# The attention part of w_out as pairs of 64-row products into two banks, both added by VectorE

## The chip, the cores and the metric

The kernel runs on one core of one Trainium2 chip. The metric is the device time of one execution in microseconds. Engines are named as in the profile: PE (TensorE), PEld (its weight loads), DVE (VectorE), ACT (ScalarE), POOL (GpSimd) and SP (SyncE, which issues nearly all the DMAs here; SPq is its queue).

## The reference

One transformer block on 1024 tokens of width 1024: a modulated norm, a projection, dilated attention beside a gated delta rule, `w_out`, and a gated FFN.

```python
def reference(x, c, w_ada, b_ada, norm_attn_g, w_in, rel_bias, conv_w, ..., w_out, norm_ffn_g, w_gate, w_up, w_down, final_norm_g):
    ...
    y_attn = _dilated_attention(...)     # 1024 x 512
    y_delta = _gated_deltanet(...)       # 1024 x 512
    y = jnp.concatenate([y_attn, y_delta], axis=-1) @ w_out[l]
    x = x + g1 * y
    h = _rmsnorm(x, norm_ffn_g[l]) * (1.0 + sc2) + sh2
    y = (jax.nn.silu(h @ w_gate[l]) * (h @ w_up[l])) @ w_down[l]
    x = x + g2 * y
    return _rmsnorm(x, final_norm_g)
```

The change touches only the rows of `w_out` that meet `y_attn`: a product of 512 inputs, 1024 outputs and 1024 tokens.

## The kernel before, in words

Everything is held transposed: features on the 128 partitions, tokens along the free axis, in two halves of 512 tokens (`hf`). A float32 product is made of three products of split operands (high part by high, high by low, low by high), so one result of 128 features by 512 tokens over 512 inputs takes 4 blocks of 128 rows times 3, that is 12 products, added up in one PSUM bank.

While the last attention heads are still at work, `out_delta` multiplies the delta half of `w_out`, adds the residual `x`, and writes the partial results to the DRAM buffer `xp`. Then comes the stage that is changed: for each half `hf` and each feature block `d` of 0 to 7 it loads the weight slab with `wsplit` (a DMA into `wr`, its high part by ACT into `wh`, its low part by POOL into `wl`), loads `xp` into the tile `x2[d, hf]`, runs the 12 products with `gemm` (line 589) and adds the result times the gate into `x2` on DVE (line 1560). The banks come in turn from the tags `g` and `s`, two of each. ACT squares `x2` (lines 1568, 1571), and POOL, or for the last two DVE, adds the squares up in `acc` (line 1572).

Two results behind, `x2_turn` (line 1483) turns `x2` back with four 128x128 transposes on PE into a bank of tag `t`; ACT copies it to `xt` (line 1485), and SP stores it (line 1486). After the eighth result of a half, `norm2` sums `acc` over the partitions (`ssq`, line 1521), takes root and reciprocal (`r`), and spreads them with a product of ones (`rsb`, line 1528, from `dg`, line 1524). For half 0 `normed2` (line 1534 on DVE, 1537 on ACT) and `h2_split` (line 1503 on ACT, 1504 on DVE) then make the operands H11 and H21 of the FFN, while PE is at half 1. Two weight slabs of the FFN's first product are loaded early into `er` (line 1543), in the buffers of `wr`.

The order on each engine is made ahead of the run by a list scheduler from priorities and dependencies; `urgent()` raises a priority, and `issue_after` sets one instruction behind another. Each engine then runs its list strictly in order and waits on semaphores.

Of the kernel before, what the change touches and what calls it, by code (L numbers as in the profile page):

```python
# [13 lines left out]
ALU = mybir.AluOpType  # L14
# [4 lines left out]
P = 128  # L19
# [63 lines left out]
def build(tc, I, out):  # L83
    nc = tc.nc
# [17 lines left out]
    def const(shape, name, dt=F32):  # L102
        return cp.tile(shape, dt, name=name, tag=name)

    def urgent():
        return tc.high_priority(offset=6000)
# [10 lines left out]
        out=tri, in_=tri, pattern=[[1, P]], compare_op=ALU.is_ge, fill=0.0,  # L117
# [28 lines left out]
    def gbank(name):  # L146
        return psb(name, "g", 2)
# [4 lines left out]
    def tbank(name):  # L152
        return psb(name, "t", 2)

    def abank(name):
        return psb(name, "a", 1)

    def ybank(name):
        return psb(name, "y", 1)
# [24 lines left out]
    mod = const([P, 48], "mod")  # L184
# [5 lines left out]
    for j in range(3):  # L190
        n = min(HALF, 1152 - HALF * j)
        ps = tbank(f"ps_R{j}")
# [30 lines left out]
    def wsplit(src, n, name, eng=None, hurry=True):  # L223
        raw = wp.tile([P, slot], F32, name=f"wr_{name}", tag="wr", bufs=3)
        hi = wp.tile([P, slot], F32R, name=f"wh_{name}", tag="wh", bufs=5)
        lo = wp.tile([P, slot], F32R, name=f"wl_{name}", tag="wl", bufs=5)
        with urgent() if hurry else ExitStack():
            nc.sync.dma_start(raw[:, :n], src)
            nc.scalar.copy(hi[:, :n], raw[:, :n])  # L229
            (eng or nc.gpsimd).tensor_tensor(  # L230
                out=lo[:, :n], in0=raw[:, :n], in1=hi[:, :n].bitcast(F32), op=ALU.subtract
            )
        return hi, lo
# [110 lines left out]
    for k in range(KT):  # L344
# [6 lines left out]
        if k == 0:  # L351
            for i in range(KT):
# [4 lines left out]
                out=G1[:, 0:1], in0=mod[:, 8:9], scalar=1.0, in1=ga[:, 0:1], op0=ALU.add, op1=ALU.mult  # L357
            )
            scaled(0, 1)
        for hf in range(2):  # L360
            cs = slice(hf * HALF, (hf + 1) * HALF)
            nc.scalar.mul(hh[k][:, cs], xts[k][:, cs], G1[:, k : k + 1])
            nc.vector.scalar_tensor_tensor(
                out=hl[k][:, cs], in0=xts[k][:, cs], scalar=G1[:, k : k + 1], in1=hh[k][:, cs].bitcast(F32),
                op0=ALU.mult, op1=ALU.subtract,
# [69 lines left out]
    for i in range(2):  # L435
        ps = aux[:, P * i : P * i + P]
# [47 lines left out]
    for hf in range(2):  # L484
        cs = slice(hf * HALF, (hf + 1) * HALF)
# [19 lines left out]
        if hf == 0:  # L505
            nc.vector.memset(pmod[3][:, 0:64], 0.0)
            for j in range(2):
                for k in range(KT):
                    w0 = slice((k % 4) * P, (k % 4 + 1) * P)
# [5 lines left out]
    for j in range(4):  # L515
        cs = slice(0, T if j < 2 else HALF)
# [42 lines left out]
    last, taken = [None], [None]  # L559
# [21 lines left out]
    def gemm(ps, slabs, mh, ml, cs):  # L581

        n = len(slabs) * 4 * 3
        i = 0
        for (wh, wl), k0 in slabs:
            for k4 in range(4):
                w0 = slice(k4 * P, (k4 + 1) * P)
                for a, b in ((wh, mh), (wh, ml), (wl, mh)):
                    last[0] = nc.tensor.matmul(ps, a[:, w0], b[k0 + k4][:, cs], start=(i == 0), stop=(i == n - 1))  # L589
                    i += 1  # L590
                yield 0.64
# [28 lines left out]
    def run(gen):  # L620
        for _w in gen:
            pass


    for q in range(2):
        ps = gbank(f"g_qd{q}")
        cs = slice(HALF, T)
# [26 lines left out]
    def v4(t):  # L654
        return t.rearrange("p (g n h) -> p g n h", g=2, n=8)
# [5 lines left out]
    for g in range(2):  # L661
        nc.vector.tensor_tensor(
            out=v4(t1)[:, g], in0=ba[:, 1, g], in1=dtb[:, 4 * g : 4 * g + 4].unsqueeze(1).to_broadcast([P, 8, 4]), op=ALU.add
# [602 lines left out]
    yh, yl = {}, {}  # L1266
# [198 lines left out]
    ps = abank("g2t")  # L1465
# [13 lines left out]
    def x2_turn(d, hf, t, bank=None):  # L1479

        ps = (bank or (abank if (hf, d % 3) == (1, 0) else tbank))(f"x2t{d}_{hf}")
        for b in range(4):
            nc.tensor.transpose(ps[:, b * P : (b + 1) * P], t[:, b * P : (b + 1) * P], ident)
        xt = px.tile([P, 4, P], F32, name=f"xt2_{d}_{hf}", tag="m", bufs=5)
        nc.scalar.copy(xt.rearrange("p b d -> p (b d)"), ps)
        nc.sync.dma_start(
            _.x2[hf][:, :, d * P : (d + 1) * P].rearrange("b p d -> p b d"), xt
        )
# [12 lines left out]
    def h2_split(name, k, src, lo_eng, copy=None):  # L1501
        hi, lo = HB[name][k]
        (copy or nc.scalar.copy)(hi, src)
        lo_eng.tensor_tensor(out=lo, in0=src, in1=hi.bitcast(F32), op=ALU.subtract)
# [27 lines left out]
    def normed2(d, hf):  # L1532
        t = x2[d, hf]
        nc.vector.scalar_tensor_tensor(
            out=t, in0=t, scalar=G2[:, d : d + 1], in1=rs, op0=ALU.mult, op1=ALU.mult
        )
        nc.scalar.activation(t, t, AF.Identity, bias=mod[:, 24 + d : 25 + d])

    def slab_early(s):
        raw = wp.tile([P, slot], F32, name=f"er{s}", tag="wr", bufs=3)  # L1540
        hi = pe.tile([P, HALF], F32R, name=f"eh{s}", tag="eh", bufs=2)
        lo = pe.tile([P, HALF], F32R, name=f"el{s}", tag="el", bufs=2)
        nc.sync.dma_start(raw, I["wg"][0, s])
        nc.scalar.copy(hi, raw)
        nc.gpsimd.tensor_tensor(out=lo, in0=raw, in1=hi.bitcast(F32), op=ALU.subtract)
        return hi, lo

    for hf in range(2):
        cs = slice(hf * HALF, (hf + 1) * HALF)
        if hf == 1:  # L1550
            acc = px.tile([P, HALF], F32, name="acc2_1", tag="m", bufs=5)
            slabs0 = [slab_early(s) for s in range(2)]
        for d in range(KT):
            slabs = [(wsplit(I["wo"][d, 0], 512, f"wo{d}_0_{hf}"), 0)]
            t = x2[d, hf]
            nc.sync.dma_start(t, _.xp[2 * d + hf])
            ps = (gbank, sbank)[d % 2](f"wo{d}_0_{hf}")
            run(gemm(ps, slabs, yh, yl, cs))
            with urgent():
                nc.vector.scalar_tensor_tensor(  # L1560
                    out=t, in0=ps, scalar=mod[:, 16 + d : 17 + d], in1=t, op0=ALU.mult, op1=ALU.add,
                )
            behind.append((d, hf, t))
            if len(behind) > 2:
                with tc.issue_after(last[0].ins):
                    x2_turn(*behind.pop(0))
            if d == 0:
                nc.scalar.activation(acc, t, AF.Square)
            else:
                sq = px.tile([P, HALF], F32, name=f"sq2_{hf}_{d}", tag="m", bufs=5)  # L1570
                nc.scalar.activation(sq, t, AF.Square)
                (nc.vector if d > 5 else nc.gpsimd).tensor_tensor(out=acc, in0=acc, in1=sq, op=ALU.add)
        if hf == 1:
            break
        while behind:
            x2_turn(*behind.pop(0))
        rs = norm2(hf, acc, ybank(f"ssq2_{hf}"), abank(f"rsb2_{hf}"))
        for d in range(KT):
            normed2(d, hf)
            h2_split(("H11", "H21")[d // 4], d % 4, x2[d, 0], nc.vector)  # L1580
# [181 lines left out]
    for k in range(4):  # L1762
# [3 lines left out]
        t = px.tile([P, HALF], F32, name=f"t2_{k}", tag="m", bufs=5)  # L1766
# [260 lines left out]
```

## Time and profile before

| | us |
|---|---|
| median of 3 runs (lowest to highest) | 1386.41 (1386.33 to 1388.37) |
| the profiled execution | 1385.31 |
| its span, first to last instruction | 1383.3 |
| granted TensorE clock, mean | 0.995 |
| DMA, share of 16 engines | 54.7% |
| changed stage, half 0: first product to the last one of `d` 7 | about 684 to 709 |
| changed stage, half 1: last product of the additions | about 739 |

A row of the timeline gives start, duration, engine, line, operation, output<-inputs, shape (rows*columns of the array, then partitions x elements), how many in a row were merged, and in brackets how long the engine was idle before and what ended the wait. Records of PE overlap: a product's duration holds its way through the array, and the distance between two starts is what one costs. A group's row gives count, busy time and mean, then idle time ahead and its releasers. Rows of stretches give the busy time and count of each engine, the granted clock, and the DMAs' share.

### The profile page before, as it was taken

How to read it: one execution, taken by the hardware profiler on the slowest of the kernel's cores; microseconds unless marked ns; L12 is line 12 of the kernel's file. 1: busy time of each engine (PE TensorE's matmuls, PEld its weight loads, DVE VectorE, ACT ScalarE, POOL GpSimd, SP SyncE). 2: the span in 40 equal slices, each digit the busy share in tenths (PEclk: the TensorE clock that was granted, in tenths of full speed). 3: DMA queues.
4: the chain of work that ended last, by engine and by line, in shares of the span. 5: the costliest groups of instructions: out<-in, count | busy, mean ns of one | idle time of the engine just before them, and what ended most of it. 6: DMA issues, size and time to landing. Idle time of an engine off the chain costs nothing.

```text
span 1383.3 us, 24383 instructions
## 1 busy us (share of the span) xinstructions
PE 1336.5 (97%) x8984; PEld 1105.9 (80%) x8984; DVE 875.4 (63%) x1678; ACT 659.7 (48%) x1285; POOL 268.4 (19%) x250
## 2 busy tenths in 40 slices
PE   8998999999999999999999999999999999999998
PEld 5777887888889877687877788888888888888876
DVE  3688583657847242766248978666675776474497
ACT  4497514347233454775168633333333333454455
POOL 2345303324213434542261000000000000000000
PEclk9999899999999999999999999999999999999999
DMA  8665574475362546531675346445453665765585
GB/s 313 228 191 171 163 212 159 138 221 164 120 175 82 170 139 178 150 100 66 211 242 168 113 154 209 142 160 175 151 177 123 218 215 183 251 226 193 191 272 192
DMA packets 169871, 245.64 MB, mean 178 GB/s; under 512 B 32566, under 2 KB 73831, under 8 KB 169752
## 3 DMA queue, kind: packets, MB, share of 16 engines
q1 hardware_dynamic: 169752, 244.08, 54.7%
q8 instruction: 71, 1.16, 0.3%
q14 instruction: 48, 0.39, 0.1%
HBM read 181.27 MB, written 67.48 MB: 180 GB/s over the span
## 4 chain that ended last, share of the span: by engine, by line
PE 71%; DVE 14%; DMA 5%; ACT 4%; issue 3%; POOL 2%; SPq 0%; POOLq 0%; DVEq 0%; ACTq 0%
PE wua L1621 9%; PE wga L1621 8%; PE X L1821 6%; PE wgc L1621 4%; PE wuc L1621 4%; PE g_a L589 4%; PE wo L589 3%; PE Z L1821 3%; PE Y L1821 2%; PE wub L1621 2%; PE wgb L1621 2%; PE y L1372 2%; PE g_va L615 2%; DVE tm L898 2%; PE f L250 2%
## 5 line engine op out<-in xcount | busy, mean ns | idle before, releaser
L1611 DVE TENSOR_TENSOR wl_db<-wr_db,wh_db 128x512 fp32r<-128x512 f32 x77 | 53.0, 691 | 67.2 <-ACT wh_db L1610 67.0
L1610 ACT CAST wh_db<-wr_db 128x512 fp32r<-128x512 f32 x77 | 47.4, 620 | 86.3 <-PE X L1821 37.8
L1331 DVE CUSTOM_DVE_ANT_0 X<-S,ng 128x512 f32<-128x512 f32 (+3 forms) x64 | 36.6, 587 | 60.9 <-PE S L1328 53.7
L1338 POOL TENSOR_SCALAR X<-X,sc 128x128 f32<-128x128 f32 (+7 forms) x64 | 48.6, 762 | 90.5 <-DVE sc L1337 77.5
L1821 PE MATMUL X<-wl_db,wh_da 128*128 128x512 f32 x160 | 62.4, 390 | 0.3 <-DVE wl_db L1611 0.3
L1821 PE MATMUL X<-wh_db,wl_da 128*128 128x512 f32 x160 | 62.3, 389 | 0.0
L1821 PE MATMUL X<-wh_db,wh_da 128*128 128x512 f32 x160 | 62.2, 389 | 0.0
L1336 ACT ACTIVATE X<-X,sc 128x128 f32<-128x128 f32 (+7 forms) x64 | 49.4, 773 | 26.7 <-DVE sc L1331 25.1
L1611 DVE TENSOR_TENSOR wl_da<-wr_da,wh_da 128x512 fp32r<-128x512 f32 x77 | 52.9, 687 | 3.5 <-ACT wh_da L1610 3.5
L1610 ACT CAST wh_da<-wr_da 128x512 fp32r<-128x512 f32 x77 | 47.4, 616 | 14.0 <-DMA wr_da<-ao_d 7.1
L589 PE MATMUL wo<-yh,wh_wo 128*128 128x512 f32 x128 | 52.0, 406 | 0.0
L589 PE MATMUL g_a<-hh,wh_a 128*128 128x512 f32 x128 | 51.4, 402 | 0.0
L589 PE MATMUL wo<-yh,wl_wo 128*128 128x512 f32 x128 | 51.1, 399 | 0.0
L589 PE MATMUL wo<-yl,wh_wo 128*128 128x512 f32 x128 | 50.6, 395 | 0.5 <-DVE yl L1439 0.5
L589 PE MATMUL g_a<-hl,wh_a 128*128 128x512 f32 x128 | 50.6, 396 | 0.0
L589 PE MATMUL g_a<-hh,wl_a 128*128 128x512 f32 x128 | 50.4, 394 | 0.0
L1351 PE MATMUL tr<-ident,X 128*128 128x128 f32 x288 | 44.1, 277 | 4.3 <-ACT et L1356 1.6
L1610 ACT CAST wh_wg_s<-wg_s 128x512 fp32r<-128x512 f32 x33 | 20.6, 623 | 56.1 <-PE wuc L1621 23.8
L1351 PEld LDWEIGHTS tr<-ident,X 128*128 128x128 f32 x288 | 32.6, 140 | 15.3 <-POOL X L1338 6.8
L1610 ACT CAST wh_wg<-wr_wg 128x512 fp32r<-128x512 f32 x31 | 19.3, 621 | 46.2 <-PE wua L1621 18.9
L1610 ACT CAST wh_wu_s<-wu_s 128x512 fp32r<-128x512 f32 x33 | 20.4, 621 | 43.6 <-PE wga L1621 17.2
L230 POOL TENSOR_TENSOR wl_wo<-wr_wo,wh_wo 128x512 fp32r<-128x512 f32 x24 | 31.8, 1326 | 48.5 <-ACT wh_wo L229 44.3
(554 smaller groups left out, 4341.9 us busy)
## 6 DMA issues: line engine op xcount, KB each, us to landing
wm<-in_wada SPq DMA_DIRECT2D x44, 512.0 KB, 6.4
wr_da<-ao_d SPq DMA_DIRECT2D x77, 256.0 KB, 2.9
wr_wu<-in_wu SPq DMA_DIRECT2D x50, 256.0 KB, 2.8
wr_wg<-in_wg SPq DMA_DIRECT2D x48, 256.0 KB, 2.9
ao_d<-a SPq DMA_DIRECT2D x44, 256.0 KB, 2.5
wr_wd<-in_wdn SPq DMA_DIRECT2D x44, 256.0 KB, 3.0
wr_db<-wt_d SPq DMA_DIRECT2D x44, 256.0 KB, 2.7
ao_d<-as SPq DMA_DIRECT2D x33, 256.0 KB, 2.0
```

The source lines that it names most:

```text
L230: (eng or nc.gpsimd).tensor_tensor(out=lo[:, :n], in0=raw[:, :n], in1=hi[:, :n].bitcast(F32), op=ALU.subtract)
L250: nc.tensor.matmul(first[bank], a[:, w0], b[k][:, cs], start=(k == 0 and n_ == 0), stop=(k == KT - 1 and n_ == 2))
L589: last[0] = nc.tensor.matmul(ps, a[:, w0], b[k0 + k4][:, cs], start=(i == 0), stop=(i == n - 1))
L615: last[0] = nc.tensor.matmul(ps[:, :n], a[k][:, ts_], b[:, w0], start=(i == 0), stop=(i == 23))
L1331: nc.vector.tensor_tensor_reduce(out=X[:, c0:c1], in0=ps[:, 0 : c1 - c0], in1=ng[:, u + c0 : u + c1], scale=1.0, scalar=(3e38 if m is None ...
L1336: nc.scalar.activation(X[:, 0:nk], X[:, 0:nk], AF.Exp, scale=-1.0, bias=m, accum_out=sc[:, 2:3])
L1338: nc.gpsimd.tensor_scalar(out=X[:, 0:nk], in0=X[:, 0:nk], scalar1=sc[:, 3:4], scalar2=0.0, op0=ALU.mult, op1=ALU.add)
L1351: nc.tensor.transpose(ps[:, (kb - c0) * P : (kb - c0 + 1) * P], X[:, kb * P : kb * P + P], ident)
L1610: nc.scalar.copy(hi, src)
L1611: (eng or nc.vector).tensor_tensor(out=lo, in0=src, in1=hi.bitcast(F32), op=ALU.subtract)
L1621: nc.tensor.matmul(ps, a[:, w0], b, start=(first and k == 0 and n_ == 0), stop=(k == 3 and n_ == 2), skip_group_check=True,)
L1821: nc.tensor.matmul(bank[b], a[:, ts_], w, start=(first and n_ == 0), stop=(last and n_ == 2), skip_group_check=True,)
```

## The change

Each 128-row product becomes two of 64 rows: rows 0 to 63 of weight and operand into a bank of tag `g`, rows 64 to 127 into a bank of tag `s`, in turn. Each bank ends with the sum over half of the inputs, and DVE adds both to `x2`, one after the other. Count by count: 192 products become 384, 16 additions on DVE become 32, and each result holds two of the four banks, not one.

```diff
+    def gemm_rows(two, slab, mh, ml, cs):
+
+        wh, wl = slab
+        i = 0
+        for k in range(4):
+            w0 = slice(k * P, (k + 1) * P)
+            for a, b in ((wh, mh), (wh, ml), (wl, mh)):
+                for e in range(2):
+                    rows = slice(64 * e, 64 * e + 64)
+                    last[0] = nc.tensor.matmul(
+                        two[e], a[rows, w0], b[k][rows, cs], start=(i == 0), stop=(i == 11)
+                    )
+                i += 1
...
             t = x2[d, hf]
             nc.sync.dma_start(t, _.xp[2 * d + hf])
-            ps = (gbank, sbank)[d % 2](f"wo{d}_0_{hf}")
-            run(gemm(ps, slabs, yh, yl, cs))
-            with urgent():
-                nc.vector.scalar_tensor_tensor(
-                    out=t, in0=ps, scalar=mod[:, 16 + d : 17 + d], in1=t, op0=ALU.mult, op1=ALU.add,
-                )
+            two = [bank_(f"wo{d}_0_{hf}_{i}") for i, bank_ in enumerate((gbank, sbank))]
+            gemm_rows(two, slabs[0][0], yh, yl, cs)
+            for ps in two:
+                with urgent():
+                    nc.vector.scalar_tensor_tensor(
+                        out=t, in0=ps, scalar=mod[:, 16 + d : 17 + d], in1=t, op0=ALU.mult, op1=ALU.add,
+                    )
```

The order of the engines changes with it. On SP, where the stage begins: `x_0_0` and its like are the tiles `x2[d, 0]`, `er` the early FFN slab. Before:

```order
L1427 DMA xp_d<-xo_1_8065 128x512
L1543 DMA er_8438<-in_wg 128x512
L1556 DMA x_0_0_8122<-xp_d 128x512
L1556 DMA x_1_0_8123<-xp_d 128x512
L1556 DMA x_2_0_8124<-xp_d 128x512
```

After:

```order
L1427 DMA xp_d<-xo_1_8065 128x512
L1570 DMA x_0_0_8122<-xp_d 128x512
L1570 DMA x_1_0_8123<-xp_d 128x512
L1570 DMA x_2_0_8124<-xp_d 128x512
L1570 DMA x_3_0_8125<-xp_d 128x512
L1570 DMA x_4_0_8134<-xp_d 128x512
L1570 DMA x_5_0_8135<-xp_d 128x512
L1570 DMA x_6_0_8136<-xp_d 128x512
L1570 DMA x_7_0_8137<-xp_d 128x512
L1543 DMA er_8550<-in_wg 128x512
```

The eight loads of `x2` have moved ahead of `er`.

On PE, between the halves: `x2t` with `x_6_0` and `x_7_0` are the last transposes of half 0, `wo_0_1` the first result of half 1, `ssq` the sum for the norm. Before:

```order
L1483 MATMUL x2t_0_8376<-ident,x_6_0_8136 128x128 x4
L589 MATMUL wo_0_1_8457<-yh_6699,wh_wo_0_1_8451 128x512
L1483 MATMUL x2t_0_8384<-ident,x_7_0_8137 128x128 x4
L589 MATMUL wo_0_1_8457<-yl_6700,wh_wo_0_1_8451 128x512
L589 MATMUL wo_0_1_8457<-yh_6699,wl_wo_0_1_8452 128x512
L589 MATMUL wo_0_1_8457<-yh_6701,wh_wo_0_1_8451 128x512
L589 MATMUL wo_0_1_8457<-yl_6702,wh_wo_0_1_8451 128x512
L1521 MATMUL ssq_0_8392<-onesr,acc_0_8121 128x1 x4
```

After:

```order
L1483 MATMUL x2t_0_8488<-ident,x_6_0_8136 128x128 x4
L1557 MATMUL wo_0_1_0_8569<-yh_6699,wh_wo_0_1_8563 128x512
L1557 MATMUL wo_0_1_1_8570<-yh_6699,wh_wo_0_1_8563 128x512
L1557 MATMUL wo_0_1_0_8569<-yl_6700,wh_wo_0_1_8563 128x512
L1483 MATMUL x2t_0_8496<-ident,x_7_0_8137 128x128 x4
L1557 MATMUL wo_0_1_1_8570<-yl_6700,wh_wo_0_1_8563 128x512
L1557 MATMUL wo_0_1_0_8569<-yh_6699,wl_wo_0_1_8564 128x512
L1557 MATMUL wo_0_1_1_8570<-yh_6699,wl_wo_0_1_8564 128x512
L1557 MATMUL wo_0_1_0_8569<-yh_6701,wh_wo_0_1_8563 128x512
L1521 MATMUL ssq_0_8504<-onesr,acc_0_8121 128x1 x4
```

The count of instructions between the transposes and the sums is nearly the same (and likewise up to `rsb`: 15 before, 12 after), but each is now half a product.

On DVE, in half 1: `x_0_0<-x_0_0,G` and its like are the normalisations of half 0, `H11l` the splits, `x_1_1<-wo` the additions of half 1. Before:

```order
L1534 SCALAR_TENSOR_TENSOR x_0_0_8122<-x_0_0_8122,G_132,rs_0_8394 128x512
L1560 SCALAR_TENSOR_TENSOR x_1_1_8127<-wo_0_1_8479,mod,x_1_1_8127 128x512
L1534 SCALAR_TENSOR_TENSOR x_1_0_8123<-x_1_0_8123,G_132,rs_0_8394 128x512
L1534 SCALAR_TENSOR_TENSOR x_2_0_8124<-x_2_0_8124,G_132,rs_0_8394 128x512
L1504 TENSOR_TENSOR H11l_8106<-x_0_0_8122,H11h_8105 128x512
L1560 SCALAR_TENSOR_TENSOR x_2_1_8128<-wo_0_1_8503,mod,x_2_1_8128 128x512
```

After:

```order
L1534 SCALAR_TENSOR_TENSOR x_0_0_8122<-x_0_0_8122,G_132,rs_0_8506 128x512
L1575 SCALAR_TENSOR_TENSOR x_0_1_8126<-wo_0_1_0_8569,mod,x_0_1_8126 128x512
L1534 SCALAR_TENSOR_TENSOR x_1_0_8123<-x_1_0_8123,G_132,rs_0_8506 128x512
L1575 SCALAR_TENSOR_TENSOR x_0_1_8126<-wo_0_1_1_8570,mod,x_0_1_8126 128x512
L1504 TENSOR_TENSOR H11l_8106<-x_0_0_8122,H11h_8105 128x512
L1534 SCALAR_TENSOR_TENSOR x_2_0_8124<-x_2_0_8124,G_132,rs_0_8506 128x512
L1504 TENSOR_TENSOR H11l_8108<-x_1_0_8123,H11h_8107 128x512
L1534 SCALAR_TENSOR_TENSOR x_3_0_8125<-x_3_0_8125,G_132,rs_0_8506 128x512
L1534 SCALAR_TENSOR_TENSOR x_4_0_8134<-x_4_0_8134,G_132,rs_0_8506 128x512
L1575 SCALAR_TENSOR_TENSOR x_1_1_8127<-wo_0_1_0_8605,mod,x_1_1_8127 128x512
L1504 TENSOR_TENSOR H11l_8110<-x_2_0_8124,H11h_8109 128x512
L1575 SCALAR_TENSOR_TENSOR x_1_1_8127<-wo_0_1_1_8606,mod,x_1_1_8127 128x512
```

Result 0 of half 1 was added ahead of this piece before; now its two additions stand among the normalisations, and those of result 1 come behind five more instructions. The two additions of result 2 follow behind another two splits and three normalisations, those of result 3 behind three splits.

## The prediction

> **What bounds the kernel now.** I read the page's busy shares and its chain that ended last, then the stretches of the changed stage, and only then single rows of the timeline.
>
> ```profile
> PE 1336.5 (97%) x8984; PEld 1105.9 (80%) x8984; DVE 875.4 (63%) x1678; ACT 659.7 (48%) x1285; POOL 268.4 (19%) x250
> PE 71%; DVE 14%; DMA 5%; ACT 4%; issue 3%; POOL 2%; SPq 0%; POOLq 0%; DVEq 0%; ACTq 0%
> 719.00:739.20 20.20, 20.20 (x98) 16.37 (x97) 18.08 (x22) 16.18 (x29) 8.67 (x6) 1.00 0.21 71
> ```
>
> PE is busy 97% of the span and holds 71% of the chain, so what it loses in the changed stage it seldom gets back. The third row is the stretch of token half 1 (start and end, length, then busy us and count of PE, PEld, DVE, ACT, POOL; granted clock 1.00). PE has no hole there, but DVE is busy 18.08 of the 20.20 us. Two limits nearly meet in this stage, and the change loads both. Below, d0 to d7 are the eight results of a half, and "a" and "b" the two additions that one result now needs.
>
> **The products.** One place of the trace already runs 64-row products in turn into two banks, line 798:
>
> ```profile
> 324.84 0.27 PE L798 MATMUL kk_q<-qd,kd 64*128 64x128 f32 x1
> 324.85 0.27 PE L798 MATMUL kk_k<-kd 64*128 64x128 f32 x1
> 324.95 0.27 PE L798 MATMUL kk_q<-qd,kd 64*128 64x128 f32 x1
> ...
> 330.10 0.28 PE L615 MATMUL g_va<-wh_va,hh 128*128 128x256 f32 x1
> 330.21 0.28 PE L615 MATMUL g_va<-wh_va,hl 128*128 128x256 f32 x1
> ```
>
> Two of them start 0.01 us apart and the next pair 0.11 later: the halves run beside each other. Whole 128-row records of the same length also start 0.11 apart (four of line 736 take 0.60 in a row below, 0.27 of it the last one's own duration). So I take a pair of halves at the price of one whole product, and the 192 pairs at nothing. The bounds: not below 512 columns' own time (products of 256 columns start 0.115 apart in the last two rows and those of 512 0.23, from 695.97 to 696.20 below, so hardly more than 0.01 is fixed, some 2 us in 192), and above, twice the price, which is a rival below.
>
> The Trainium skill, page "TensorE: Matmul & The Clock Gate", section "Measured speedup vs the span model", has four 32-row tiles of 512 columns run 3.07 times as fast, not 4. By it, as an estimate, a pair would cost 1.10 of a whole product and this stage some 3 us more; no run here shows pairs of 512 columns.
>
> **Each change of shape costs.** The transposes `x2t` stay 128-row and stand between the 64-row products.
>
> ```profile
> 317.10 0.60 PE L736 MATMUL trk_0True<-ident,kd 128*128 128x128 f32 x4
> 317.63 0.49 PE L798 MATMUL kk_q<-qd,kd 64*128 64x128 f32 x4
> 318.05 0.66 PE L736 MATMUL trk_1True<-ident,kd 128*128 128x128 f32 x4
> 473.61 0.39 PE L589 MATMUL g_a<-hl,wh_a 128*128 128x512 f32 x1
> 473.93 0.88 PE L1372 MATMUL y<-et,va 128*64 128x128 f32 x12
> 474.74 0.50 PE L589 MATMUL g_a<-hh,wl_a 128*128 128x512 f32 x1
> 475.07 0.39 PE L589 MATMUL g_a<-hh,wh_a 128*128 128x512 f32 x1
> 695.97 0.39 PE L589 MATMUL wo<-yh,wl_wo 128*128 128x512 f32 x1
> 696.20 0.60 PE L1483 MATMUL x2t<-ident,x 128*128 128x128 f32 x4
> 696.55 0.48 PE L589 MATMUL wo<-yh,wh_wo 128*128 128x512 f32 x1
> 696.87 0.40 PE L589 MATMUL wo<-yl,wh_wo 128*128 128x512 f32 x1
> ```
>
> The last `trk` starts at 317.10 + 0.60 - 0.27 = 317.43 and the first `kk_q` at 317.63: 0.20 where 0.11 is normal; the same 0.20 on the way back, and the four transposes then take 0.66, not 0.60. Around 512-column products another change of shape (line 1372) shows the rest: 0.32 into it (473.61 to 473.93), 0.20 out, and 0.33 for the first product after it. One visit to `x2t` today takes from 695.97 to 696.87, 0.90 us. With changes: 0.32 + (0.66 - 0.27) + 0.20 + 0.33 = 1.24, so **+0.34 a visit**, and a result's period goes from 3.22 (four from this `x2t` at 696.20 to that at 709.06, below) to 3.55. Half 0 has five such visits.
>
> **The banks go round faster.** Four banks held four results; now each result takes one of both tags, and d2 needs d0's.
>
> ```profile
> 686.60 0.32 SPq L1427 DMA_DIRECT2D xp_d<-xo  x1
> 688.75 0.33 SPq L1543 DMA_DIRECT2D er<-in_wg  x1
> 689.17 3.23 SPq L1556 DMA_DIRECT2D x<-xp_d  x7
> 692.16 0.75 DVE L1560 SCALAR_TENSOR_TENSOR x<-wo,mod,x 128x512 f32<-128x512 f32 x1 [5.59 <-PE wo L589]
> 692.96 0.66 PE L1483 MATMUL x2t<-ident,x 128*128 128x128 f32 x4 [0.63 <-DVE x L1560]
> ```
>
> d0's products are long done at 692.16; its `x` lands then, issued at 689.17 because `er` stood ahead of it on SP until 688.75. Afterwards `x` stands ahead of `er` and goes out behind `xp_d`, near 686.92: 2.25 earlier. So d0's a starts at 689.9 and b ends at 691.3 (0.75 each, 0.67 net of overlap). PE has done d0 and d1 by 689.7 and must wait: the second half of d2's first product starts at 691.3, 2.7 us of products follow, and the first `x2t` comes at 694.1, not 692.96: **+1.1**. With five visits (+1.7) half 0 ends at 711.9, not 709.06 (the first row below).
>
> **Between the halves.**
>
> ```profile
> 709.06 1.03 PE L1483 MATMUL x2t<-ident,x 128*128 128x128 f32 x8
> 713.21 1.05 PE L1521 MATMUL ssq<-onesr,acc 128*128 128x1 f32 x8 [0.58 <-DVE acc L1572]
> 718.48 1.12 PE L1528 MATMUL rsb<-dg,onesr 128*128 128x512 f32 x2 [0.71 <-DVE dg L1524]
> 716.00 0.75 DVE L1560 SCALAR_TENSOR_TENSOR x<-wo,mod,x 128x512 f32<-128x512 f32 x1 [2.85 <-PE wo L589]
> 716.67 0.17 DVE L1523 RECIPROCAL r<-r 128x4 f32<-128x4 f32 x1
> 716.87 1.56 DVE L1524 TENSOR_TENSOR dg<-ident,r 128x512 f32<-128x512 f32 x1
> ```
>
> `ssq` needs d7's a and b, the square and the sum: 711.9 + 0.1 + 1.42 + 0.63 + 0.69, with waits between engines about 715.2 (before 713.21). From `ssq` to `rsb` it is 5.27 us today, 0.67 of it because the reciprocal stood behind half 1's first addition; in the new order it stands ahead, and `dg`'s 1.56 may fall towards the 0.69 of the splits of this size (below). I take 4.2 (between 3.7 and 5.3): `rsb` at 719.4, **+0.9**. But PE uses the wait worse. The order puts about as many instructions there as before, 19 against 20, and each is half a product. So 10.5 products more are left for later, 2.4 us.
>
> **Half 1: DVE becomes the bound.**
>
> ```profile
> L1534 DVE SCALAR_TENSOR_TENSOR x<-x,G,rs 128x512 f32<-128x512 f32 x8 | 8.4, 1083 | 1.8 <-ACT rs L1529 1.8
> L1560 DVE SCALAR_TENSOR_TENSOR x<-wo,mod,x 128x512 f32<-128x512 f32 x6 | 4.5, 742 | 0.0
> L1504 DVE TENSOR_TENSOR H11l<-x,H11h 128x512 fp32r<-128x512 f32 x4 | 3.7, 953 | 0.0
> L1504 DVE TENSOR_TENSOR H21l<-x,H21h 128x512 fp32r<-128x512 f32 x4 | 2.6, 685 | 0.6 <-ACT H21h L1503 0.6
> ```
>
> These are DVE's instructions from 719 to 740. Net of overlap I take 1.0 us for a normalisation (n), 0.75 for a split (s), 0.67 for an addition, and follow the new order from R, the start of `rsb`; DVE starts 1.8 behind it, as now (720.26). n, d0a, n, d0b end at R+5.2; s, n, s, n, n, d1a, s, d1b at R+11.7; two s, three n, d2a, d2b at R+17.6; three s, d3a, d3b at R+21.2. PE may start d3 behind d1b, d4 behind d2b, d5 behind d3b: it would be ready about R+8.6, R+15.2 and R+21.0. So d5 starts at R+21.2, and three results of 3.55, less the last visit, end at R+31.0. Today it is 20.7, from 718.48 to the end of the stretch quoted first. **+10.3.** The bounds: with n and s at 0.67, d5 could start at R+18.0 (end R+27.8); were DVE never waited for, the products and changes alone end at R+25.2.
>
> **After it.** The additions end at 750.4 against 739.2, +11.2 in sum.
>
> ```profile
> 743.68 1.05 PE L1521 MATMUL ssq<-onesr,acc 128*128 128x1 f32 x8 [0.87 <-DVE acc L1572]
> PEld wua L1621 <- ACT wh_wu_s L1610: 1.7, 1, 1.7
> ```
>
> The second `ssq` waits 0.87 now, since POOL's sums ran late there; in a slower stage they are done, and the wait goes (-0.9). The later wait of 1.7 hangs on DVE and ACT, which are now ahead of PE: I take half of it back (-0.8). PE then bounds to the end and the rest stays. **Sum: +11.2 - 0.9 - 0.8 = +9.5.** The profiled execution took 1385.31 (span 1383.3, the remainder around it), so 1394.8; the median of the runs, 1386.41, lies 1.1 above it: **1395.9**.
>
> **Rivals.** *The halves run one after the other.* Line 798's records hold 128 columns in 0.11, half the rate of the 512-column products, so two full-rate streams are not shown. Each of 16 results would cost 2.7 us more, 43.6, less the waits for DVE that then vanish (5.8) and d2's (1): about 1433. Chance 9%.
>
> *The clock falls.* A wait of PE long enough halves it:
>
> ```profile
> 131.00:134.00 3.00, 0.30 (x2) 0.00 (x0) 2.96 (x5) 0.00 (x0) 1.25 (x1) 1.00 0.24 81
> 136.00:138.00 2.00, 2.00 (x18) 2.00 (x17) 1.94 (x3) 2.00 (x9) 2.00 (x2) 0.50 1.13 271
> 142.00:146.00 4.00, 4.00 (x44) 4.00 (x42) 2.38 (x4) 4.00 (x11) 0.49 (x1) 0.59 0.41 128
> 259.01 0.46 PE L997 MATMUL st<-S,kd 128*128 128x128 f32 x2 [2.08 <-DVE S L1032]
> ```
>
> After an empty stretch of 2.7 us the clock was 0.50 until about 145.3 (0.59 over the last stretch is 3.3 of its 4 us at half), some 10 us that lose 5; a wait of 2.08 did nothing. Mine are 1.5 to 2.2 before `rsb` and 1.7 before d3. If one grows past 2.7: about 1401. Chance 8%. (The Trainium skill, same page, section "HAM oscillation — how this bites in real kernels", puts the gap at over 3.4 us; here 2.7 sufficed, and the measurement decides.)
>
> *Within 0.2%.* DVE is not waited for, as its order is met with slack, and most changes of shape fall into waits that exist anyway: 11.2 - 5.8 - 3 and the two gains, about 1387 to 1389. Chance 7%.
>
> *Faster, by the pairs.* The two tiles cover each other's fixed 0.01 and their changes of shape: -2.0, and `x`, which lands 2.25 earlier, saves the 0.63 wait, the second `ssq` wait goes too (-0.9): about 1382.9. It decides only if a pair starts every 0.216 and a change costs nothing; the 0.20 rows speak against it. Chance 4%.
>
> **Numbers.** The forecast has 72%. Its own range: DVE's short durations (-3.2) and the 1.7 wait gone wholly (-0.9) give 1391.8; `rsb` may come 0.5 earlier or 1.1 later, and nothing may come back of the 0.8; a microsecond for what I rounded: 1390.5 to 1399. To reach 8 in 10 the upper end takes in the fallen clock: 1390.5 to 1402. A measurement of this kernel tells about 0.2%, 2.8 us, from no change. Faster 4%, same 7%, slower 89%.
>
> **What would show it.** Halves of a pair starting within 0.02 us and pairs 0.23 apart; 0.32 into and 0.20 out of `x2t`; the first two products of d2 in half 0 waiting for DVE; in half 1 PE idle ahead of d3 and d4, ended by the additions, and DVE without holes; `rsb` near 719 and the last addition product near 750. I am wrong if pairs start 0.45 apart, if a clock of 0.50 stands in this stage, or if DVE finishes half 1's additions as PE delivers them.

## The result, and the profile after

| | median, us | lowest to highest |
|---|---|---|
| before, 4 runs | 1386.76 | 1386.33 to 1388.37 |
| after, 4 runs | 1400.98 | 1398.99 to 1411.06 |

The changed kernel is slower: ratio 1.0104, 95% interval 1.0074 to 1.0134, that is 14.2 us. The profiled execution is the slowest of the four (span 1408.9); it lost about 8 us ahead of the changed stage, in code that the change leaves as it was, where its clock stood at 0.50 three times (at 259.43, 392.55 and 587.11, 20.5 us in all). A second profile (run "again", below) has none of these. So times inside the stage are told from its first product on, which stands at 683.89 before, at 692.11 here and at 681.86 in "again".

Busy times and the chain of the page, after:

```profile
PE 1357.7 (96%) x9176; PEld 1117.8 (79%) x9176; DVE 885.8 (63%) x1694; ACT 660.6 (47%) x1285; POOL 266.3 (19%) x250
PE 71%; DVE 13%; DMA 6%; ACT 3%; issue 3%; POOL 1%; SPq 0%; DVEq 0%; ACTq 0%; POOLq 0%
```

192 more instructions on PE and 16 more on DVE, and PE still bounds. PE's timeline in half 0, after (where two are merged in a row, it is a pair):

```profile
692.45 0.40 PE L1557 MATMUL wo<-yl,wh_wo 64*128 64x512 f32 x2
692.68 0.39 PE L1557 MATMUL wo<-yh,wl_wo 64*128 64x512 f32 x2
...
700.90 0.47 PE L1557 MATMUL wo<-yh,wh_wo 64*128 64x512 f32 x1 [3.06 <-DVE x L1575]
701.66 0.49 PE L1557 MATMUL wo<-yh,wh_wo 64*128 64x512 f32 x1 [0.29 <-DVE x L1575]
...
707.85 0.39 PE L1557 MATMUL wo<-yh,wl_wo 64*128 64x512 f32 x2
708.17 0.66 PE L1483 MATMUL x2t<-ident,x 128*128 128x128 f32 x4
708.76 0.50 PE L1557 MATMUL wo<-yh,wh_wo 64*128 64x512 f32 x2
709.09 0.40 PE L1557 MATMUL wo<-yl,wh_wo 64*128 64x512 f32 x2
```

Pairs stand 0.23 apart. From 707.85 to 709.09 a visit to `x2t` takes 1.24, where it took 0.90. And `d` 2 waits for DVE, 3.06 and 0.29, since DVE itself waited for `x`. The stretches of the whole stage and, below each, of its half 1, before and then after (start and end, length, busy us and count of PE, PEld, DVE, ACT, POOL, granted clock, DMA share, GB/s):

```profile
683.89:738.97 55.08, 52.40 (x255) 42.12 (x254) 28.83 (x36) 34.00 (x61) 30.50 (x23) 1.00 0.61 194
718.48:738.97 20.49, 20.49 (x97) 16.53 (x98) 18.07 (x22) 15.96 (x29) 8.44 (x6) 1.00 0.24 79
```

```profile
692.11:761.62 69.51, 61.89 (x447) 44.67 (x446) 39.13 (x52) 35.77 (x62) 31.60 (x24) 0.95 0.52 160
730.35:761.62 31.27, 27.90 (x197) 20.00 (x195) 23.36 (x31) 19.05 (x32) 11.08 (x8) 0.94 0.15 44
```

The stage has grown by 14.4. Half 1, from `rsb` to the last addition product (second rows), takes 31.27 instead of 20.49, and PE idles for 3.4 of them. The clock is no longer 1.00: in 6.8 us of the stage it was 0.50.

### The profile page after: what moved, and what is told of

Read it like the earlier page. It is cut to its first block, busy times and chain, and to the rows that moved or that the text cites. A ratio compares the mean times of both kernels' runs of the same rounds, so it can differ in the third digit from the quotient of the medians.

```text
span 1408.9 us, 24800 instructions
## 1 busy us (share of the span) xinstructions
PE 1357.7 (96%) x9176; PEld 1117.8 (79%) x9176; DVE 885.8 (63%) x1694; ACT 660.6 (47%) x1285; POOL 266.3 (19%) x250
## 4 chain that ended last, share of the span: by engine, by line
PE 71%; DVE 13%; DMA 6%; ACT 3%; issue 3%; POOL 1%; SPq 0%; DVEq 0%; ACTq 0%; POOLq 0%
PE wua L1636 9%; PE wga L1636 8%; PE X L1836 6%; PE wuc L1636 4%; PE g_a L589 4%; PE wgc L1636 4%; PE wo L589 3%; PE Z L1836 3%; PE y L1372 2%; PE g_va L615 2%; PE Y L1836 2%; PE wgb L1636 2%; DVE tt L902 2%; PE tr L1351 2%; PE wub L1636 2%
## 5 line engine op out<-in xcount | busy, mean ns | idle before, releaser
L1836 PE MATMUL X<-wl_db,wh_da 128*128 128x512 f32 x160 | 62.4, 390 | 0.3 <-DVE wl_db L1626 0.3
L1625 ACT CAST wh_wg_s<-wg_s 128x512 fp32r<-128x512 f32 x33 | 20.5, 622 | 58.0 <-PE wuc L1636 24.5
L1557 PE MATMUL wo<-yh,wh_wo 64*128 64x512 f32 x128 | 35.3, 431 | 6.7 <-DVE x L1575 6.7
L615 PE MATMUL g_va<-wl_va,hh 128*128 128x256 f32 x128 | 39.3, 307 | 0.0
L615 PE MATMUL g_va<-wh_va,hh 128*128 128x256 f32 x128 | 39.3, 307 | 0.0
```

The source lines that it names most:

```text
L615: last[0] = nc.tensor.matmul(ps[:, :n], a[k][:, ts_], b[:, w0], start=(i == 0), stop=(i == 23))
L1557: last[0] = nc.tensor.matmul(two[e], a[rows, w0], b[k][rows, cs], start=(i == 0), stop=(i == 11))
L1625: nc.scalar.copy(hi, src)
L1836: nc.tensor.matmul(bank[b], a[:, ts_], w, start=(first and n_ == 0), stop=(last and n_ == 2), skip_group_check=True,)
```

## The experiments

The theory, A: four terms carry the loss, that is changes of shape around `x2t`, the wait of `d` 2 in half 0, DVE in half 1, and a clock that falls while PE waits. Rivals: the pairs or the additions themselves, or one term alone. In the table, "stage" is the length from the first to the last addition product in the profile; "half clock" is how much of it ran at 0.50, and half of that is lost if PE had work all the time. A median comes from 4 to 12 executions ("block" had one), but waits and falls are seen in the one that was profiled, so what ties a median to a wait rests on one execution of each kernel.

| run | median (before beside it), us | ratio, 95% interval | stage | half clock |
|---|---|---|---|---|
| before | | | 55.1 | 0 |
| again | 1399.30 (1386.70) | 1.0082 (1.0061 to 1.0104) | 67.6 | 6.8 |
| whole | 1392.01 (1386.70) | 1.0035 (1.0019 to 1.0050) | 58.3 | 3.4 |
| whole6 | 1389.64 (1385.44) | 1.0019 (1.0004 to 1.0034) | 55.4 | 0 |
| block | 1412.31, one run | | 84.9 | 0 |
| xlate | 1405.19 (1386.70) | 1.0128 (1.0103 to 1.0153) | 73.1 | 10.2 |
| order1 | 1396.07 (1385.44) | 1.0071 (1.0051 to 1.0092) | 63.0 | 6.8 |
| banks6 | 1402.43 (1385.44) | 1.0113 (1.0091 to 1.0135) | 70.1 | 13.7 |
| both | 1396.68 (1385.44) | 1.0069 (1.0048 to 1.0090) | 65.0 | 10.2 |
| turn64 | 1398.27 (1386.74) | 1.0084 (1.0071 to 1.0098) | 61.9 | 10.2 |
| spare | 1395.64 (1386.74) | 1.0068 (1.0054 to 1.0082) | 65.8 | 10.2 |
| seam | 1393.97 (1388.05) | 1.0040 (1.0018 to 1.0061) | 62.4 | 3.4 |
| seam64 | 1393.71 (1388.05) | 1.0038 (1.0021 to 1.0055) | 59.2 | 0 |

### again: the changed kernel once more

> The changed kernel once more. Theory A (four terms: changes of shape around x2t, d2's wait for DVE in half 0, DVE as the bound of half 1, and falls of the clock in those waits): 1399 to 1402 us; with 2 or 3 half-clock windows in the stage or behind it (1.7 us each) and none before the stage, so a shorter profiled execution than 1411. Rival (the three early falls belong to the change): they come again at about 259, 393 and 587 us.

Stretches of "again": the stage, half 1, and two windows in it.

```profile
681.86:749.45 67.59, 61.88 (x446) 44.22 (x446) 38.95 (x52) 35.87 (x62) 31.41 (x24) 0.95 0.51 163
689.85:693.26 3.41, 3.41 (x18) 2.68 (x18) 1.50 (x2) 1.46 (x3) 2.23 (x2) 0.50 1.05 399
718.53:749.45 30.92, 27.70 (x194) 19.44 (x195) 23.39 (x31) 19.05 (x32) 11.12 (x8) 0.94 0.15 46
734.22:737.63 3.41, 3.22 (x13) 2.16 (x15) 3.28 (x5) 3.37 (x7) 1.49 (x2) 0.50 0.22 64
```

And the waits of PE beside them, with the rows of SP and DVE ahead of the first:

```profile
684.56 4.05 SPq L1570 DMA_DIRECT2D x<-xp_d  x8
687.90 1.61 DVE L1575 SCALAR_TENSOR_TENSOR x<-wo,mod,x 128x512 f32<-128x512 f32 x2 [4.58 <-DMA x<-xp_d]
688.80 0.47 PE L1557 MATMUL wo<-yh,wh_wo 64*128 64x512 f32 x1 [1.21 <-DVE x L1575]
689.56 0.57 PE L1557 MATMUL wo<-yh,wh_wo 64*128 64x512 f32 x1 [0.29 <-DVE x L1575]
...
728.74 0.49 PE L1557 MATMUL wo<-yh,wh_wo 64*128 64x512 f32 x1 [0.77 <-DVE x L1575]
734.05 0.66 PE L1557 MATMUL wo<-yh,wh_wo 64*128 64x512 f32 x1 [1.70 <-DVE x L1575]
```

As A expected: no early falls, two in the stage, each right behind a wait for DVE (1.21 with 0.29, and 1.70). They cost 2 x 1.7. Over five runs the clock's mean was 0.992 at the median against 0.995 of the kernel before; 0.003 of 1397 is 4.2 of the 12.6 us, if PE had work in those times; where the clock fell in the runs without a profile is not known.

### whole and whole6: no change of shape

```diff
-                for e in range(2):
-                    rows = slice(64 * e, 64 * e + 64)
-                    last[0] = nc.tensor.matmul(
-                        two[e], a[rows, w0], b[k][rows, cs], start=(i == 0), stop=(i == 11)
-                    )
+                last[0] = nc.tensor.matmul(
+                    two[k // 2], a[:, w0], b[k][:, cs], start=(i % 6 == 0), stop=(i % 6 == 5)
+                )
```

> 128-row products again, the first six of a result into a bank of tag g, the last six into one of tag s; two additions as in the change. So no change of shape, but the same banks and additions. Theory A: x2t stands 3.22 us apart in half 0 (not 3.55), d2 of half 0 still waits about 3 us for DVE, half 1 still waits for additions; 14 visits at 0.33 = 4.6 us come back: about 1396 us (1392 to 1398). Rival 1 (the changes of shape are nearly all of it): about 1387. Rival 2 (shape is nothing, banks and additions all): 1400 to 1402.

> 128-row products, first six and last six into two banks, both added, and three pairs of banks in turn. Theory A (banks are all that was left of the loss in the 128-row version): x2t of half 0 where the kernel before has them, no fall of the clock in the stage: 1385 to 1388 us, that is the 16 further additions are free. Rival (the additions cost by themselves): 1390 to 1392, as with two pairs.

PE's timeline of "whole", then its stretch of half 1:

```profile
694.32 0.47 PE L1555 MATMUL wo<-yh,wh_wo 128*128 128x512 f32 x1 [3.59 <-DVE x L1573]
...
705.19 0.60 PE L1483 MATMUL x2t<-ident,x 128*128 128x128 f32 x4
708.41 0.60 PE L1483 MATMUL x2t<-ident,x 128*128 128x128 f32 x4
```

```profile
722.83:743.32 20.49, 20.49 (x98) 16.54 (x98) 19.31 (x24) 14.50 (x26) 9.60 (x7) 1.00 0.14 43
```

`x2t` is 3.22 apart again and `d` 2 still waits, as A said. But half 1 takes 20.49, to the digit what it took before, though DVE does the same 16 additions: A had expected waits there, and that part of it fell. The time, 1392, is the low end of A. What differs from the changed kernel on DVE is the order: here each result's additions stand between one or two normalisations or splits, there behind up to five. But here the first bank of a result is also complete half a result earlier than with the pairs, so this run alone does not show that the order did it; "order1" below does. With a third pair of banks ("whole6", the edit under "banks6") the stage is 55.41 and the clock 1.00, so two banks and 16 additions cost it 0.3. Behind the stage stands a wait that the kernel before does not have:

```profile
743.88 0.50 PE L1634 MATMUL wga<-H11h,eh 128*128 128x512 f32 x1 [1.82 <-ACT xt L1485]
```

The FFN's first product waits 1.82 for a copy of ACT, and the clock falls for 3.41 us behind it. So the version with the additions is not quite free: 4.2 us between the medians, interval 0.04% to 0.34%. Its 1389.64 lies above A's 1385 to 1388 and just below the rival's 1390 to 1392.

### block: the halves not in turn

```diff
 
         wh, wl = slab
-        i = 0
-        for k in range(4):
-            w0 = slice(k * P, (k + 1) * P)
-            for a, b in ((wh, mh), (wh, ml), (wl, mh)):
-                for e in range(2):
-                    rows = slice(64 * e, 64 * e + 64)
+        for e in range(2):
+            rows = slice(64 * e, 64 * e + 64)
+            i = 0
+            for k in range(4):
+                w0 = slice(k * P, (k + 1) * P)
+                for a, b in ((wh, mh), (wh, ml), (wl, mh)):
                     last[0] = nc.tensor.matmul(
                         two[e], a[rows, w0], b[k][rows, cs], start=(i == 0), stop=(i == 11)
                     )
-                i += 1
+                    i += 1
 
     for hf in range(2):
```

> For each result the 12 products of rows 0 to 63, then the 12 of rows 64 to 127, not in turn. Theory A (halves are cheap because the two of a pair run at the same time): products of one half start 0.227 us apart, so a result takes 24 x 0.227 = 5.45 us, not 2.72; 16 results add 43.6, less the waits for DVE that then vanish (some 8): 1430 to 1440 us. Rival (64 rows take half the time by themselves): starts 0.113 apart and no change, about 1401.

PE's timeline of "block" where one half of a result ends and the other begins:

```profile
702.48 0.40 PE L1557 MATMUL wo<-yh,wh_wo 64*128 64x512 f32 x1
702.72 0.39 PE L1557 MATMUL wo<-yl,wh_wo 64*128 64x512 f32 x1
702.95 0.39 PE L1557 MATMUL wo<-yh,wl_wo 64*128 64x512 f32 x1
702.95 0.62 PE L1557 MATMUL wo<-yh,wh_wo 64*128 64x512 f32 x2
703.29 0.51 PE L1557 MATMUL wo<-yl,wh_wo 64*128 64x512 f32 x2
703.52 0.50 PE L1557 MATMUL wo<-yh,wl_wo 64*128 64x512 f32 x2
703.75 0.39 PE L1557 MATMUL wo<-yh,wh_wo 64*128 64x512 f32 x1
```

A single half costs 0.23, as much as a whole product: the pair is cheap because its two run at the same time. That decides against the rival (0.113 apart, 1401), but the 1412.31 lies 18 us below A's range too: against the changed kernel, where A has some 35 (43.6 - 8), the stage grew by only 15.4. Around the seam eight products start within 0.81 us: those of the second half begin beside the last of the first. So `x2t` stands 5.49 apart, and not 24 x 0.227 and 0.83 for the visit, 6.28; over 16 results that is some 13 us. The kernel's text sets the two halves one behind the other; whether the scheduler's list on PE does so too is not on record, so who moved these products stays open. PE is idle for 0.6 us in the whole stage, and the clock stays at 1.00.

### xlate: fewer loads beside the first `x`

```diff
-            nc.sync.dma_start(t, _.xp[2 * d + hf])
...
+                if d > 1:
+                    nc.scalar.copy(x2[e][:, 0:1], gates[d - 2][:, 0:1])
+                nc.sync.dma_start(x2[e], _.xp[2 * e[0] + e[1]])
```

(`e` is result `d` of half 0 and one of half 1, `gates` the first banks of the results.)

> The x loads of d2 and later, and of half 1, wait for a one-column copy of ACT, so only x of d0 and d1 and one er load go out at first. Theory A1 (x of d0 lands 5 us after its issue because seven more loads share the 16 engines with it): it lands about 3 us after its issue, d2's wait of 3.06 falls to about 1, and the time by some 2 us, to 1398 or 1399. Rival A2 (x of d0 stands behind the write of xp_d issued 0.4 us before it): it lands 5 us after its issue as before, d2 waits 3 us, and the time stays at 1401.

The issue and the first addition, of the changed kernel and then of "xlate":

```profile
694.81 4.42 SPq L1570 DMA_DIRECT2D x<-xp_d  x8
700.00 2.27 DVE L1575 SCALAR_TENSOR_TENSOR x<-wo,mod,x 128x512 f32<-128x512 f32 x3 [5.95 <-DMA x<-xp_d]
```

```profile
688.40 0.95 SPq L1575 DMA_DIRECT2D x<-xp_d  x2
692.76 3.12 DVE L1581 SCALAR_TENSOR_TENSOR x<-wo,mod,x 128x512 f32<-128x512 f32 x4 [4.76 <-DMA x<-xp_d]
```

From issue to use it is 5.19, here 4.36 with two loads, and in "again" 3.34 with eight. Neither A1 nor A2 holds: the same program has 3.34 and 5.19. What spreads it stays open. The edit itself made the kernel slower: DVE now waits for later loads (4.74 and 1.93 us in half 0), and the first product of `d` 2 waits 2.60, up to the edit's own copy on ACT, which itself stands behind DVE's first addition.

### order1: the additions ahead on DVE

```diff
...
+            if hf == 1 and d < 7:
+                with tc.issue_after(added.ins):
+                    for k in ((0, 1), (2,), (3,), (4,), (5,), (6,), (7,))[d]:
+                        normed2(k, 0)
+                    for k in ((), (0,), (1,), (2,), (3,), (4,), (5, 6, 7))[d]:
+                        h2_split(("H11", "H21")[k // 4], k % 4, x2[k, 0], nc.vector)
...
-        for d in range(KT):
-            normed2(d, hf)
-            h2_split(("H11", "H21")[d // 4], d % 4, x2[d, 0], nc.vector)
```

> The changed kernel, but on DVE in half 1 each result's two additions stand ahead of the normalisations and splits, which are spread one of each behind every result (3.1 us of DVE work in a result of 3.55). Theory A (the order on DVE, not the amount of its work, makes half 1 late): from rsb to the last addition product 23 to 24 us instead of 30.9, no wait for DVE over 0.5 us there and no fall of the clock: 1390 to 1393 us. Rival (the amount of DVE work, 16 more additions, is the bound of half 1): still 29 or more, 1397 to 1400.

(`added` is the second addition of a result.) In "again" three normalisations stood on DVE ahead of the additions of result 2, whose banks result 4 needs, so that PE waited 1.70:

```profile
730.23 3.10 DVE L1534 SCALAR_TENSOR_TENSOR x<-x,G,rs 128x512 f32<-128x512 f32 x3
733.26 1.59 DVE L1575 SCALAR_TENSOR_TENSOR x<-wo,mod,x 128x512 f32<-128x512 f32 x2
```

Stretch of half 1 in "order1":

```profile
722.89:747.74 24.85, 24.85 (x193) 18.23 (x195) 21.42 (x29) 18.91 (x32) 12.23 (x8) 1.00 0.21 63
```

No hole on PE, no fall: 24.85 instead of 30.92, of which 1.7 is the clock and 4.4 the order. So the order of DVE's work, not its amount, made half 1 wait. The 24.85 are near the R+25.2 that the prediction gave for products and changes of shape without a wait. The median fell by less than expected, by 2.0 against before beside it, with intervals that overlap, and 1396.07 lies between A's range and the rival's: in the profile `d` 2's wait (2.48 here) brought 6.8 us at half clock.

### banks6 and both: three pairs of banks

```diff
-        ps = (bank or (abank if (hf, d % 3) == (1, 0) else tbank))(f"x2t{d}_{hf}")
+        ps = (bank or tbank)(f"x2t{d}_{hf}")
-            two = [... enumerate((gbank, sbank))]
+            two = [... enumerate((abank, ybank) if d % 3 == 2 else (gbank, sbank))]
```

"both" adds the edit of order1.

> The changed kernel with three pairs of banks in turn (d2 and d5 of both halves into the two single banks, which the norm and some transposes used), x2t always in tag t; DVE's order as in the change. Theory A (the banks make PE wait): in half 0 d2 starts without a wait and the fall of the clock behind it goes, -3 to -5; in half 1 the wait moves one result on and shrinks, -2 to -3: 1392 to 1395 us. Rival (x of the first results bounds anyway, one result later): half 0 ends where it did, and only half 1 gains: 1396 to 1398.

> Both edits: three pairs of banks and the additions ahead on DVE. Theory A: only the changes of shape are left, 14 visits at 0.33 us less what falls into waits that exist anyway: 1388 to 1391 us, and no fall of the clock in the stage. Rival (a pair costs more than a whole product somewhere that these traces do not show): 1393 or more.

PE and DVE in "banks6":

```profile
700.85 0.66 PE L1483 MATMUL x2t<-ident,x 128*128 128x128 f32 x4 [1.46 <-ACT xt L1485]
...
712.91 1.57 DVE L1587 TENSOR_TENSOR acc<-acc,sq 128x512 f32<-128x512 f32 x1 [3.26 <-ACT sq L1586]
...
716.14 1.08 PE L1483 MATMUL x2t<-ident,x 128*128 128x128 f32 x4 [2.50 <-DVE x L1575]
```

`d` 2 starts without a wait, and the first `x2t` stands 8.61 behind the stage's start (12.24 in "again", 9.07 before). Then PE waits 1.46 for ACT, and at the end of half 0 2.50 for `d` 7's additions, which stand on DVE behind a sum that waits 3.26 for ACT's square. In that wait the clock falls, for 10.24 us. For "banks6" neither A nor the rival holds (1402.43 is above both). "both" missed A's 1388 to 1391 and lies in the rival's range, but its profile has another reason than the rival's: a wait of 2.49 at the end of half 0 and 10.24 us at half clock, which cost up to 5.1. What one wait gave, the next and the clock took back, in both kernels.

### turn64: no change of shape, with the pairs

This run, "spare" and "seam" have the edit of order1 too, so they are compared with it.

```diff
...
+            for b in range(4):
+                for e in range(2):
+                    r = slice(64 * e, 64 * e + 64)
+                    nc.tensor.transpose(pair[e][:, b * 64 : b * 64 + 64], t[r, b * P : (b + 1) * P], ident[r, r])
+            for e in range(2):
+                nc.scalar.copy(xt[:, :, 64 * e : 64 * e + 64], pair[e][:, 0:256].rearrange("p (b d) -> p b d", b=4))
```

> As the kernel with the additions ahead on DVE (order1), and x2t too is turned back in pairs of 64-row transposes, into two banks, so that no shape changes from the first product of a half to its norm; ACT copies two halves of 256 columns. Theory A (the change of shape costs 0.33 a visit): x2t stands 3.2 us apart or less in half 0 instead of 3.55, from rsb to the last addition product 23 us instead of 24.85, and the time falls by 3 to 4.5 us against order1, to 1391.5 to 1393. Rival (64-row products cost 0.33 a result more whatever stands beside them): 3.5 apart, 1396.

Two visits in half 0 of "turn64", and its stretches of half 1 and between the halves:

```profile
705.24 0.28 PE L1492 MATMUL x2t<-ident,x 64*128 64x64 f32 x2
...
708.31 0.28 PE L1492 MATMUL x2t<-ident,x 64*128 64x64 f32 x2
```

```profile
719.78:726.61 6.83, 6.83 (x28) 4.76 (x28) 0.87 (x2) 2.81 (x5) 0.00 (x0) 0.50 0.55 152
725.73:748.46 22.73, 22.73 (x214) 19.33 (x214) 19.99 (x27) 18.00 (x35) 12.28 (x8) 0.98 0.16 48
```

`x2t` stands 3.07 apart, not 3.55, and half 1 takes 22.73, not 24.85, so the rival falls. Of the 0.48, "whole" shows 0.33 for the shape; the rest comes with the other transposes. Yet the time did not fall: 1398.27 is above A's range. PE came sooner to the end of half 0 and waited there 1.58 for DVE, and 6.83 us at half clock followed; 3.41 more came behind 1.44 at `d` 2.

### spare: work in the wait of `d` 2

```diff
+            if (hf, d) == (0, 2):
+                spare = tbank("spare")
+                with tc.issue_after(last[0].ins):
+                    for k in range(8):
+                        nc.tensor.matmul(spare, slabs[0][0][0][:, 0:P], yh[k % 4][:, cs], start=(k == 0), stop=(k == 7))
```

> As order1, with eight products of 128 rows more, into a bank that nobody reads, between d1 and d2 of half 0, where PE waits for DVE. They take some 2.2 us with the changes of shape; the wait there has been 1.2 to 3.6. Theory A (PE's idle time there makes the clock fall): no fall in the 10 us behind d2's start, and the time 1 to 3 us below order1's, 1393 to 1395. Rival (the clock falls for another reason, the halves' start for one): a fall there all the same, and 1396 to 1398.

PE in "spare", and the stretch between the halves:

```profile
690.72 2.12 PE L1576 MATMUL spare<-yh,wh_wo 128*128 128x512 f32 x8
695.82 0.66 PE L1483 MATMUL x2t<-ident,x 128*128 128x128 f32 x4
...
718.24 1.09 PE L1483 MATMUL x2t<-ident,x 128*128 128x128 f32 x4 [2.90 <-DVE x L1580]
```

```profile
716.86:727.10 10.24, 8.86 (x32) 5.37 (x32) 2.69 (x5) 3.23 (x5) 0.84 (x1) 0.50 0.59 157
```

PE is busy through `d` 2's start and no fall follows there, as A said (in one profile; the first one after had none there either, with a wait of 3.06); the first `x2t` stands 10.77 behind the stage's start. The next long wait, 2.90 at the end of half 0, has the fall instead, and the ratio is order1's; 1395.64 is just above A's 1393 to 1395.

### seam and seam64: more products between the halves

"seam" splits `norm2` and sets its parts behind products of half 1:

```diff
...
-        while behind:
-            x2_turn(*behind.pop(0))
-        rs = norm2(hf, acc, ybank(f"ssq2_{hf}"), abank(f"rsb2_{hf}"))
...
+            if (hf, d) == (1, 0):
+                with tc.issue_after(last[0].ins):
+                    x2_turn(*seam[0])
+                first_added = added
+            if (hf, d) == (1, 1):
+                rs, dg, pb = norm2_sum(0, seam[1], ybank("ssq2_0"), abank("rsb2_0"), fourth[0], first_added)
+            if (hf, d) == (1, 2):
+                norm2_spread(rs, dg, pb, fourth[0])
...
```

"seam64" adds the edits of turn64 and spare.

> As order1, and between the halves PE runs all of d0 and a third of d1 of half 1 before ssq, and two thirds of d1 and a third of d2 before rsb (28 pairs in all, instead of 12), with d0's additions ahead of the reciprocal on DVE. Theory A (pairs are half as long as the order between the halves supposes, so PE waits there and the clock falls): no wait over 1 us between the halves, no fall there, and the last addition product 3 to 4 us earlier against the stage's start than in order1: 1392 to 1394 us. Rival (the time between the halves is set by the norm's own chain through DVE and ACT): the wait moves behind rsb, to d3, and the time stays at 1395 to 1397.

> All edits that took a wait or a change of shape away: the additions ahead on DVE, more products between the halves, x2t as pairs of 64-row transposes, and the eight spare products before d2 of half 0. Theory A (changes of shape, orders made for longer products, and the clock in the waits are the whole loss): within 4 us of the kernel before, 1387 to 1391 us, x2t 3.07 us apart, no fall of the clock in the stage. Rival (something of the loss lies in the pairs or the additions themselves): 1392 or more.

PE in "seam", then in "seam64", and the latter's stage:

```profile
698.58 0.47 PE L1584 MATMUL wo<-yh,wh_wo 64*128 64x512 f32 x1 [3.07 <-DVE x L1603]
```

```profile
702.32 0.27 PE L1492 MATMUL x2u<-ident,x 64*128 64x64 f32 x1 [2.42 <-ACT xt L1494]
```

```profile
685.78:744.97 59.19, 54.29 (x506) 46.93 (x507) 35.28 (x49) 35.21 (x74) 32.08 (x24) 1.00 0.59 185
```

In "seam" the wait of 3.07 at `d` 2 is the only one above 1.2 us, and one window at half clock follows it. By the medians it gained, as A said (1.0040 against order1's 1.0071, with intervals that overlap); by the profiles its stage is only 0.5 shorter than order1's, though 3.4 us less of it ran at half clock, and order1's profile happened to have no wait between the halves. So what this edit is worth by itself stays open. "seam64" has no fall in the stage, which is still 4.1 us longer than before: 2.42 and 1.61 are waits for ACT's copies, which its own edits brought. Its 1393.71 missed A's range and lies in the rival's (1392 or more); the two waits account for the stage, but that the additions or the pairs cost something behind it, as in "whole6", is not excluded. No version with pairs came near the kernel before, and nothing here beats it.

## Why the prediction was right, and where it was short

Slower was right, and 1400.98 lies inside the range, near its upper end; the forecast of 1395.9 is 5.1 short. It is inside only because the upper end took in the fallen clock: the forecast's own range ended at 1399. And one of the prediction's own signs of being wrong came true, a clock of 0.50 in this stage.

- **Products.** Right: pairs 0.23 apart, and "block" shows that the two run at the same time. The 1.10 that came from the Trainium skill, page "TensorE: Matmul & The Clock Gate", section "Measured speedup vs the span model", does not show in these pairs. (As an estimate by it, 192 pairs of 0.23 would have cost 4.4 us more, not some 3.)
- **Changes of shape.** Right to the digit: 1.24 a visit, 3.55 a result. "whole" takes them away (3.22), "turn64" too (3.07).
- **The banks in half 0.** The wait of `d` 2 came as forecast: 1.21 and 0.29 in "again", against 1.6 (689.7 to 691.3). The first addition stood 6.04 behind the stage's start in "again" (forecast 689.9 - 683.89 = 6.0), but 7.89 in the first profile, whose `d` 2 then waited 3.06: the 3.0 us taken for the landing of `x` held in one execution (3.34) and not in the other (5.19). The first `x2t` came 3.2 later than before in "again" (forecast +1.1), 1.7 of it by the clock.
- **Between the halves.** Forecast +0.9 at `rsb` against the stage's start. Measured 34.59 before, 36.67 in "again", of which 1.7 is the clock: +0.4 without it. In the first profile +3.7: the late `x` is 1.85 of it, and a window at half clock (727.06 to 730.47) lies ahead of `rsb` here too.
- **Half 1.** Forecast 31.0; measured 30.92 and 31.27, with 1.7 of clock in each, so 29.2 and 29.6, inside its bounds. PE waited ahead of d3 and d4, as the order said, and DVE had no hole until d3's additions; but the waits in "again" were 1.0 and 1.9, where the sum has 3.1 (R+8.6 to R+11.7) and 2.4. The heading "DVE becomes the bound" was half the truth. The same work in another order ("order1", "whole") makes PE wait for nothing.
- **After it.** The second `ssq` gained its 0.9 (from +12.5 to +11.6 in "again"); the 0.8 of the later wait did not come (+12.4 at the end).
- **The clock.** This is the step that failed: "Mine are 1.5 to 2.2 before `rsb` and 1.7 before d3. If one grows past 2.7", with a chance of 8% and 5 us. The wait before `rsb` was 0.82 in "again", and falls came behind waits of 1.21 and 1.70 elsewhere, in windows of 3.41 us that cost 1.7 each. The "1.7 before d3" is not what the prediction's own sum has there (3.1, above its 2.7), and the row by which "a wait of 2.08 did nothing" was luck: the same wait at L997, 2.08 to 2.14 long, stands near 259 in four other profiles, and in three of them ("xlate", "order1", "turn64") the clock falls in it or 0.1 behind it. As an estimate, the 4.2 us of the medians' clock and the forecast's +9.5 make 13.7, beside 12.6 and 14.2 measured.

Without the clock "again" ends at +12.4 - 3.4 = +9.0, against +9.5. That the two are so close is partly luck: half 1 was forecast 1.6 too long (+10.3 against 29.2 - 20.49 = +8.7) and `rsb` 0.5 too late, and the later wait, from which 0.8 was to come back, took 0.8 more.

## What to carry to other kernels

A change can cost little by its own instructions and much by an order on another engine that no longer fits: look where each engine's queue puts the work that PE waits for, and test the order alone before blaming the load. Where short waits of PE can bring microseconds at half clock, look for every wait over a microsecond, and at how much of a few microseconds around it PE is idle, not only for the longest wait; taking one away helps only if the next one does not open. Halves of the rows in turn cost no more than whole products, but each visit to an instruction of another shape does, here 0.33 us.

## What the runs showed of the hardware

- **The clock.** All its falls in and near the stage last 3.41 us or two or three times that. Between 681 and 775 us the profiles of all kernels hold 23 waits of PE of 1.2 us or more; 16 have a fall that begins in the wait or within 2.2 us of its end, and only one of 17 falls (at 727.06 in the first profile after) has none, but a wait of 0.89. "before" and "block" have no such wait and no fall there. 7 waits, one of 3.06 among them, brought none. In each profile the falls begin and end on one grid of 3.413-us steps (counted from its own falls), and they go with the idle share of one step more than with the length of a wait. Of the steps at full clock between 681 and 775 us, all 8 in which PE was busy for less than 43% are followed by half clock, 8 of 12 from 43% to 57%, and 1 of 328 above. The wait of 3.06 lay across two steps (busy 1.50 and 1.97 of 3.41 us, that is 44% and 58%); the wait of 1.21 lay with its 0.29 in one (1.91, that is 56%). What decides in the middle stays open. The Trainium skill, page "TensorE: Matmul & The Clock Gate", section "What's actually happening", has a free-running window of 3413 ns, which the lengths agree with; that a whole idle window is needed to fall, as its table of states has it, is not borne out here.
- **Single halves.** A 64-row product of 512 columns holds 0.23 us alone, as a 128-row one does, and products of the other half start beside it: in turn in the changed kernel, and around the seam in "block", whose text does not set them in turn.
- **A change of shape.** The Trainium skill, page "TensorEngine Tiling (Array Packing)", section "Key Properties", says that a change of tiling mode drains the engine; the runs price the way there and back around four transposes at 0.33 us.
- **Loads.** The same program's `x` took 3.34 us from issue to use in one execution, and 5.19 in another.
